# Queries and keys of heads 2 and 3 made by column block inside the attention, instead of in a second pass ahead of the values

## The chip, the cores and the metric

The kernel runs on one core of one Trainium2 chip. The metric is the device time of one execution in microseconds (us). Engines are named as in the profile: PE (TensorE), PEld (its weight loads), DVE (VectorE), ACT (ScalarE), POOL (GpSimd), SP (SyncE, which issues most of the DMAs). Lines such as L449 are lines of the kernel before; where a line belongs to the changed kernel, the text says so.

## What is computed

The reference is a network of two layers on 512 rows of x and 256 rows of ctx, 1024 features each. Only the mixer of the even layer is touched by the change. Cut to what matters, it is:

```python
u, v, q, k, vv = split(h @ w_in)            # h: normed and modulated rows; u, v, q, k, vv: 512 columns each
q, k = rope(q), rope(k)                     # 8 query and 8 key heads of 64 (rope on the rows of x only)
s = einsum(q, k) * HEAD_DIM ** -0.5
p = softmax(s)                              # 4 heads, each with two softmaxes
a = p[:, :, 0] - lam * p[:, :, 1]
o = a @ vv
y = concat([chunk_mlp(u, v), rmsnorm(o) * g]) @ w_out   # chunk_mlp: gelu, norm and mixing of blocks of 128 rows
```

The scale and shift that modulate h, and four more of each layer, come from products of a condition vector with a large matrix, `ada`.

## The kernel before

Every product is made in three matmuls (`mm3`, L106, L107, L108): the weight and the activation are both split into a high part and a rest, and hi*hi, hi*rest and rest*hi are summed. So each weight tile that comes by DMA (`unit`, L73) is cast on ACT (`CAST w<-raw`, L81), and POOL takes the rest (L84).

PSUM (where PE's results land) has eight banks. In this layer they are two `wide` tiles of two banks each (`pw` in the profile), three single banks (`pb`) and one bank called `fill` (`pf`). A new tile of one of these tags waits until all readers of the old one in its place are done.

The even layer, `even()`, goes on as follows. The numbers of time are those of the profiled execution.

- Start to 39.17 us: x, the first slabs of `ada`, norm.
- L449, loop `half`: for half 0 the queries and keys of heads 0 and 1, four blocks of 128 columns, all four at once over the eight tiles of the inner dimension: first for the 512 rows of x into two wide tiles, then for the 256 rows of ctx into two single banks. ACT moves them out (`evacuate`, L440). Then half 1, the same for heads 2 and 3 (81.28 to 122.24 us). Rope runs on DVE and POOL.
- L497 to L512: the values, eight tiles of the inner dimension with six accumulators each (122.24 to 162.87 us). ACT and DVE split them (`vhi`, `vlo`, L122 and L123).
- Sixteen slabs of `ada` (columns for j=2 and j=4, 1 MB each) are used on the side: `ada_ahead` issues the DMA, `ada_some` makes the eight small matmuls of one step (L359; the profile shows four or eight in a row), and after eight steps one copy on ACT (L366, `t`) and transposes (L368). Six steps stand in half 1, six in the values.
- Attention, `head(t)` for t = 0 to 3: three blocks of 256 rows, for each of which two `softmax_diff` of 128 rows are made. One of these takes two wide tiles: products (L542, L543, `pw<-kh,qa` and the like), row maximum on DVE (L544), exponential on ACT (L546, `e`), difference on DVE (L552). Then transposes (L564), their split on ACT and DVE (L122 `ath`, L123 `atl`) and the products with the values. The stacked and split queries and keys that a head needs (`stack`: L261, L262, L276, L277 on ACT, L265 and L279 on DVE) are made in the head before it.
- Filling: `gated(i)` makes one column block of u or v, 24 matmuls of 512 into the fill bank, a copy on ACT (L585), 24 of 256 into the same bank, a copy. The four blocks i = 4 to 7 (v) stand between the steps of heads 0 and 1. Their gelus (L632) are held behind the last exponential of head 1, since the two functions need different tables on ACT (`ACT_TABLE_LOAD`). Heads 2 and 3 are held behind the last gelu. They are filled by `turn(g)` (transposes of v, L644, copies, L645, and statistics, L648 and L649) and `gated(0)` to `gated(3)`, so `gated(0)` comes after the first `turn`.
- `mix` and the output product follow, then the feed-forward part and the odd layer, which the change leaves alone.

The order of the work on each engine is fixed when the program is built: a scheduler takes the ready instruction of highest priority. `tc.high_priority` sets a piece ahead of others, and `issue_after` holds it behind a named instruction. At run time each engine goes through its own list in order and waits for semaphores. SP's list of DMAs is such a list too, and a DMA waits there until the memory it writes is free.

Of the kernel before, what the change touches and what calls it, by code (L numbers as in the profile page):

```python
# [6 lines left out]
F32 = mybir.dt.float32  # L7
# [19 lines left out]
class Builder:  # L27
# [220 lines left out]
    def rope(self, ps, out, tabs):  # L248
        nc = self.nc
        sh = self.ropep.tile([P, 512], F32, name=self.uid("sh"), tag="sh", bufs=2)  # L250
# [71 lines left out]
    def even(self):  # L322
        tc, nc, a = self.tc, self.nc, self.a
        self.open_ring(512, 5, 6)
        self.adap = tc.alloc_tile_pool(name="ada0", bufs=1, side="left", reuse_waits="tile")
        self.ropep = tc.alloc_tile_pool(name="rope0", bufs=1, side="left", reuse_waits="tile")
# [111 lines left out]
        tabs = []  # L438

        def evacuate(ps, n, c, heads):  # L440
            h = heads[n % 2]
            key = h if n < 2 else 4 + h
            if key not in qk:
                qk[key] = f3()
            nc.scalar.mul(qk[key][:, c], ps, 0.125 if n < 2 else 1.0)
# [3 lines left out]
        for half, heads in enumerate(((0, 1), (2, 3))):  # L449
            w2 = [self.wide(), self.wide()]  # L450
            accx = [w[:, h * 512:(h + 1) * 512] for w in w2 for h in range(2)]
            W = []
            for k in range(KT):
                t = self.adap.tile([P, 2, 512], F32R, name=self.uid("wq"), tag="wq", bufs=3) if k % 3 == 2 else None
                with tc.issue_after(self.last_slab.ins) if half == 0 else ExitStack():
                    W.append(self.blocks(a["qk"][half, k], 512, t=t))
                    if half == 0:
                        if k > 4:
                            with tc.issue_after(self.last_w.ins):
                                ada_ahead(1)  # L460
                        if k == 7:
                            tabs += [self.load(self.ropep, a[n], [P, TX], n) for n in ("cos", "sin")]
                if half == 0:
                    t, sh = hx[k], self.modcol(0, 0, k, 0)
                    nc.scalar.activation(axx[k][0], t, AF.Identity, bias=sh)
                    nc.vector.scalar_tensor_tensor(axx[k][1], t, sh, axx[k][0].bitcast(F32), ALU.add, ALU.subtract)
                elif k % 2:
                    ada_ahead(1)
                    ada_some()
                for n in range(4):  # L470
                    self.mm3(accx[n], W[k][n], axx[k], k == 0, k == KT - 1)
                if half == 0 and k == 4:
                    rd = self.rstd_diag([(self.squares(hc, TC), TC)], 1.0 / D)[0]
                if half == 0 and k == 5:
                    rc = self.spread(rd)
                    for i in range(KT):
                        self.modulate(hc[i], TC, self.modcol(0, 1, i, 1), self.modcol(0, 0, i, 1), rc, axc[i])
            for n in range(4):
                evacuate(accx[n], n, slice(0, TX), heads)
            bk = [self.bank() for _ in range(2)]  # L480
            accc = [b[:, h * TC:(h + 1) * TC] for b in bk for h in range(2)]
            for k in range(KT):
                for n in range(4):
                    self.mm3(accc[n], W[k][n], axc[k], k == 0 and n % 2 == 0, k == KT - 1)
                if k % 2 and k > 2 - half:
                    ada_ahead(1)
                    ada_some()
            for n in range(4):
                evacuate(accc[n], n, slice(TX, TA), heads)
            for h in heads:  # L490
                for n in (h, 4 + h):
                    self.rope(qk[n][:, :TX], qk[n][:, :TX], tabs)
# [7 lines left out]
        for k in range(KT):  # L500
            W = self.unit(a["v0"][k * P:(k + 1) * P, :], 512)
            for tb in range(6):
                c = slice(tb * P, (tb + 1) * P)
                self.mm3(acc[tb], [t[:, c] for t in AX_[k]], W, k == 0, k == KT - 1)
            ada_ahead(1)
            ada_some()
# [12 lines left out]
        here = tc.cur_priority  # L519
        self.ropep.release()  # L520
# [10 lines left out]
        def softmax_diff(Q, K, qb, eps):  # L531
# [6 lines left out]
            for c in range(2):  # L538
# [6 lines left out]
                e = Ra.tile([P, TA], F32, name=self.uid("e"), tag="e", bufs=6)  # L545
# [120 lines left out]

        with tc.high_priority(offset=tc.cur_priority - here):
            QK = {0: stack(0)}
        for t in range(2):
            head(t)  # L670
# [12 lines left out]
        Ra.release()  # L683
        self.close_ring()
# [818 lines left out]
def prep(inp):  # L1503
# [18 lines left out]
    r["qk"] = c(ew[:, 1024:2048].reshape(KT, P, 2, 2, 2 * P).transpose(3, 0, 1, 2, 4).reshape(2, KT, P, 512))  # L1522
# [5 lines left out]

    r["uv"] = cols(ew[:, 0:1024])
# [44 lines left out]
```

## Time and profile before

| what | value |
|---|---|
| median of 3 runs | 1590.26 us (1588.08 to 1591.02) |
| profiled execution | 1588.33 us, its span 1586.3 us |
| mean granted clock of PE | 0.988 |
| PE busy | 1518.7 us (96%) |
| DVE, ACT, POOL busy | 1084.7, 723.3, 830.7 us |
| PE busy from 39 to 333 us (the span of the even mixer) | 275.60 us of 294.00 |

A table of windows shows, for each stretch, its length, the busy time of each engine with the number of its instructions in brackets, the granted clock of PE as a share of the full one, the busy share of the DMA engines and their GB/s. A table of waits has, for one engine, the instruction that waited and the one it waited for (after the arrow), the time in all, how often, and the longest. A timeline has the start, the length, engine, line and operation of each instruction with output and inputs, and in square brackets the idle time before it and what ended it.

### The profile page before, as it was taken

To read this page: it belongs to the slowest core of one execution; us is meant where nothing else is said; L and a number is where in the kernel's file an instruction comes from. 1 tells how busy PE (TensorE), PEld (TensorE's weight loads), DVE (VectorE), ACT (ScalarE), POOL (GpSimd) and SP (SyncE) were. 2 spreads that over 40 slices of the span, in tenths; PEclk is the share of its full clock that TensorE was granted. 3 is DMA by queue.
4 is the path that set the end of the run, shared out by engine and by line. 5 is a ranking of instruction groups with operands and counts; after the bars stand their busy time and mean duration, and the time that the engine had idled before them with its cause. 6 is when DMAs were issued, how large, how long until landed. Compare 5 with 4: busy or idle time off the path is not lost.

```text
span 1586.3 us, 24984 instructions
## 1 busy us (share of the span) xinstructions
PE 1518.7 (96%) x9547; PEld 1352.2 (85%) x9547; DVE 1084.7 (68%) x1958; ACT 723.3 (46%) x1472; POOL 830.7 (52%) x565
## 2 busy tenths in 40 slices
PE   6999988999999999999999989999999999999996
PEld 4776877889989999999999978777869989999996
DVE  4720788765688788888785585765667976666656
ACT  2412676553552333333333244565655644444443
POOL 0463211061256776677676415531304398888883
PEclk9999999999999999999999999999999999999998
DMA  8845100033223333454451012110225132323301
GB/s 328 308 145 188 40 8 1 3 131 133 67 80 113 114 120 106 140 166 147 164 165 57 27 52 80 61 34 14 68 80 206 54 120 88 113 92 109 94 14 54
DMA packets 54295, 162.00 MB, mean 102 GB/s; under 512 B 6176, under 2 KB 10656, under 8 KB 46496
## 3 DMA queue, kind: packets, MB, share of 16 engines
q1 hardware_dynamic: 47120, 135.11, 25.5%
q10 hardware_dynamic: 7056, 25.30, 4.9%
q8 instruction: 75, 1.23, 0.3%
q14 instruction: 44, 0.36, 0.1%
HBM read 158.29 MB, written 2.10 MB: 101 GB/s over the span
## 4 chain that ended last, share of the span: by engine, by line
PE 83%; DVE 10%; ACT 3%; issue 2%; DMA 1%; POOL 0%; POOLq 0%; SPq 0%; DVEq 0%; ACTq 0%
PE pw L106 11%; PE pw L107 11%; PE pw L108 11%; PE pb L107 8%; PE pb L106 8%; PE pb L108 8%; PE pf L106 4%; PE pf L107 4%; PE pf L108 4%; PE pb L1427 2%; PE pb L1416 2%; PE pf L359 2%; PE pw L1379 1%; PE pw L1387 1%; PE pw L542 1%
## 5 line engine op out<-in xcount | busy, mean ns | idle before, releaser
L84 POOL TENSOR_TENSOR w<-raw,w 128x512 fp32r<-128x512 f32 (+1 forms) x84 | 127.5, 1525 | 242.9 <-ACT w L81 220.5
L107 PE MATMUL pw<-ax,w 128*128 128x384 f32 (+2 forms) x732 | 233.9, 320 | 3.7 <-DVE ax L201 2.3
L106 PE MATMUL pw<-ax,w 128*128 128x384 f32 (+2 forms) x732 | 232.9, 322 | 4.1 <-DVE q L879 1.9
L108 PE MATMUL pw<-ax,w 128*128 128x384 f32 (+2 forms) x732 | 233.1, 320 | 0.1
L774 DVE SCALAR_TENSOR_TENSOR xT<-pb,mod,xT 128x512 f32<-128x512 f32 (+3 forms) x208 | 145.7, 707 | 125.8 <-PE pb L108 125.5
L879 POOL TENSOR_TENSOR w<-raw,w 128x512 fp32r<-128x512 f32 x110 | 169.4, 1555 | 19.7 <-ACT w L879 19.5
L879 POOL TENSOR_TENSOR w<-t,w 128x512 fp32r<-128x512 f32 x99 | 148.6, 1504 | 55.6 <-ACT w L879 55.6
L106 PE MATMUL pb<-hh,w 128*128 128x512 f32 x480 | 171.0, 356 | 2.3 <-DVE xT L774 2.3
L108 PE MATMUL pb<-hh,w 128*128 128x512 f32 x480 | 171.5, 357 | 0.3 <-DVE w L879 0.3
L107 PE MATMUL pb<-hh,w 128*128 128x512 f32 x480 | 171.1, 356 | 0.0
L107 PE MATMUL pw<-T,w 128*128 128x384 f32 (+1 forms) x508 | 156.9, 310 | 1.2 <-DVE T L123 1.2
L106 PE MATMUL pw<-T,w 128*128 128x384 f32 (+1 forms) x508 | 156.3, 310 | 1.1 <-DVE hs L879 1.1
L108 PE MATMUL pw<-T,w 128*128 128x384 f32 (+1 forms) x508 | 157.0, 310 | 0.0
L106 PEld LDWEIGHTS pw<-ax,w 128*128 128x128 f32 x732 | 138.5, 190 | 12.5 <-DVE q L879 2.6
L107 PEld LDWEIGHTS pw<-ax,w 128*128 128x128 f32 x732 | 139.0, 190 | 11.2 <-DVE ax L201 3.6
L106 PE MATMUL pf<-ax,w 128*128 128x256 f32 (+2 forms) x420 | 139.9, 333 | 7.9 <-DVE qf L252 5.0
L108 PEld LDWEIGHTS pw<-ax,w 128*128 128x128 f32 x732 | 139.2, 190 | 3.1 <-DVE w L948 0.4
L107 PE MATMUL pf<-ax,w 128*128 128x256 f32 (+2 forms) x420 | 138.8, 330 | 0.0
L108 PE MATMUL pf<-ax,w 128*128 128x256 f32 (+2 forms) x420 | 138.7, 330 | 0.0
L879 POOL TENSOR_TENSOR hh<-hs,hh 128x768 fp32r<-128x768 f32 (+1 forms) x42 | 80.7, 1922 | 90.0 <-ACT hh L879 67.6
L879 POOL TENSOR_TENSOR w<-rawo,w 128x512 fp32r<-128x512 f32 x59 | 103.5, 1754 | 30.1 <-ACT w L879 30.1
L228 DVE SCALAR_TENSOR_TENSOR junk<-ar,cb 128x1024 bf16<-128x1024 f32 x64 | 105.6, 1651 | 0.0
(378 smaller groups left out, 3936.8 us busy)
## 6 DMA issues: line engine op xcount, KB each, us to landing
raw<-ffn_in SPq DMA_DIRECT2D x44, 1024.0 KB, 5.1
ar<-ada SPq DMA_DIRECT2D x24, 1024.0 KB, 6.9
ar<-ada ACTq DMA_DIRECT2D x48, 512.0 KB, 3.5
rawo<-ffn_out SPq DMA_DIRECT2D x88, 256.0 KB, 3.0
raw<-odd_out SPq DMA_DIRECT2D x32, 256.0 KB, 2.7
raw<-qk SPq DMA_DIRECT2D x16, 256.0 KB, 7.9
raw<-uv SPq DMA_DIRECT2D x16, 256.0 KB, 2.7
raw<-even_out SPq DMA_DIRECT2D x8, 512.0 KB, 3.5
```

Source lines behind the costliest of these rows:

```text
L84: eng.tensor_tensor(lo, raw, hi.bitcast(F32), ALU.subtract)
L106: mm(out, s[0], m[0], start=start, stop=False, **kw)
L107: mm(out, s[0], m[1], start=False, stop=False, **kw)
L108: return mm(out, s[1], m[0], start=False, stop=stop, **kw)
L228: return self.nc.vector.scalar_tensor_tensor(junk, t, 1.0, self.cb[who], ALU.mult, ALU.mult, accum_out=self.acc[who][:, col:col + 1])
L359: nc.tensor.matmul(ps[32 * q:32 * q + 32, :w], cst[:, k, :], t[:, w * q:w * q + w], start=k == 0, stop=k == KT - 1, skip_group_check=True)
L542: nc.tensor.matmul(ps[:, :TX], Q[c][:, qs], K[c][p][:, :TX], start=p == 0, stop=p == 1)
L774: ins = self.nc.vector.scalar_tensor_tensor(h, ps[:, r], self.modcol(l, j, m, who), h, ALU.mult, ALU.add)
L879: tail[key] = fn(*args, **kw)
L1379: nc.tensor.matmul(ps[:, st:en], Q, K[g][p][:, b0 * P:b1 * P], start=p == 0, stop=p == 1, skip_group_check=True)
L1416: last = nc.tensor.transpose(pt[:, x * P:(x + 1) * P], es[2 * (x % 2) + x // 2][:, kb * P:(kb + 1) * P], self.ident)
L1427: nc.tensor.matmul(po[64 * h:64 * h + 64, :], V[vb][:, 64 * g:64 * g + 64], t[:, h * TC:h * TC + TC], start=kb == 0, stop=kb == nb - 1, sk ...
```

## The change

The loop over `half` is gone. What was half 0 stays, and the values follow it directly. Heads 2 and 3 get their queries and keys as four column blocks (order 2, 6, 3, 7: query of head 2, key of head 2, and so on), each made like a `gated` block: 24 matmuls of 512 into the fill bank, out by ACT (L445 of the changed kernel), 24 of 256, out by ACT, rope. They have lower priority than heads 0 and 1 and higher than `gated(4)` to `gated(7)`, so they are the first filling of heads 0 and 1. Weights are laid out to fit on the host, in `prep`. Twelve of the sixteen `ada` steps now stand in the values (one or two for each tile of the inner dimension), four in half 0. Since rope runs inside the attention, its tables and its buffer stay allocated until the attention is over, and three buffers are made smaller: `sh` from 2 to 1, `e` from 6 to 5, `wq` from 3 to 2. The numbers of instructions and of DMAs on each engine are the same as before.

```diff
-        for half, heads in enumerate(((0, 1), (2, 3))):
...
-                if half == 0:
-                    t, sh = hx[k], self.modcol(0, 0, k, 0)
...
-                elif k % 2:
-                    ada_ahead(1)
-                    ada_some()
...
+        keys = (0, 1, 4, 5)
+        W = []
+        for k in range(KT):
+            t = self.adap.tile([P, 2, 512], F32R, name=self.uid("wq"), tag="wq", bufs=2) if k in (2, 5) else None
+            with tc.issue_after(self.last_slab.ins):
+                W.append(self.blocks(a["qk"][k], 512, t=t))
+                if k > 3:
+                    with tc.issue_after(self.last_w.ins):
+                        ada_ahead(1)
...
@@ values
-            ada_ahead(1)
-            ada_some()
+            for _ in range(1 + k % 2):
+                ada_some()
+                ada_ahead(1)
...
-        here = tc.cur_priority
-        self.ropep.release()
         self.adap.release()
...
-                e = Ra.tile([P, TA], F32, name=self.uid("e"), tag="e", bufs=6)
+                e = Ra.tile([P, TA], F32, name=self.uid("e"), tag="e", bufs=5)
...
+        here = tc.cur_priority
+        for n, key in enumerate((2, 6, 3, 7)):
+            W = self.blocks(a["qk1"][n])
+            qk[key] = f3()
+            for c, A in ((slice(0, TX), axx), (slice(TX, TA), axc)):
+                ps = self.fill()[:, :c.stop - c.start]
+                self.dense(ps, W, A)
+                evacuate(ps, key, c)
+            self.rope(qk[key][:, :TX], qk[key][:, :TX], tabs)
         with tc.high_priority(offset=tc.cur_priority - here):
             QK = {0: stack(0)}
-        for t in range(2):
-            head(t)
+            for t in range(2):
+                head(t)
```

How the order moves is shown at three places. The numbers at the ends of names tell buffers apart and differ between the two kernels. First ACT at the end of the values, before: the last copy of `ada` (`t_1218`) and then the stacks of head 0 (`qa_1322` to `kh_1334`), and only then the values (`vhi`).

```order
L366 COPY t_1218<-pf_982 128x512
L261 ACTIVATE qa_1322<-f_102_572 64x768
L262 ACTIVATE qb_1323<-f_102_572 64x768
L276 CAST kh_1328<-f_104_576 64x768
L277 CAST kh_1328<-f_104_576 64x768
L261 ACTIVATE qa_1528<-f_103_574 64x768
L276 CAST kh_1334<-f_104_576 64x768
L277 CAST kh_1334<-f_104_576 64x768
L81 CAST w_2031<-raw_2029 128x512
L276 CAST kh_1534<-f_105_578 64x768
L277 CAST kh_1534<-f_105_578 64x768
L122 CAST vhi_1274<-pw_1045 128x512
```

The same place on ACT in the changed kernel, where `f_160` is the query block of head 2:

```order
L122 CAST vhi_1027<-pb_737 128x512
L81 CAST w_1197<-raw_1195 128x512
L122 CAST vhi_1019<-pw_735 128x512
L369 COPY t_997<-pf_863 128x512
L261 ACTIVATE qa_1326<-f_56_330 64x768
L262 ACTIVATE qb_1327<-f_56_330 64x768
L276 CAST kh_1332<-f_57_331 64x768
L277 CAST kh_1332<-f_57_331 64x768
L261 ACTIVATE qa_1532<-f_58_332 64x768
L276 CAST kh_1338<-f_57_331 64x768
...
L445 ACTIVATE f_160_1064<-pf_1065 128x512
...
L540 ACTIVATE e_1354,sa_1347<-pw_1348,sa_1346 128x768
```

The values' casts now stand ahead of the last `ada` copy and of the stacks, and the first evacuation of a filling product stands behind the stacks (three more rows of stacks stand in the first gap, one weight cast in the second).

Second, PE where the filling of head 1 ends. Before, the last four matmuls of `gated(7)` (`pf_2129`) have head 1's products with the values and its next scores behind them:

```order
L108 MATMUL pf_2129<-ax_323,w_2099 128x256
L106 MATMUL pf_2129<-ax_325,w_2099 128x256
L107 MATMUL pf_2129<-ax_326,w_2099 128x256
L108 MATMUL pf_2129<-ax_325,w_2099 128x256
L107 MATMUL pb_1651<-atl_1673,vhi_1282 128x256
L108 MATMUL pb_1651<-ath_1672,vlo_1283 128x256
L106 MATMUL pb_1651<-ath_1672,vhi_1286 128x256
...
L156 MATMUL pb_1699<-ones,sq_1601 128x128 x4
L543 MATMUL pw_1848<-kh_1534,qa_1528 128x256
```

In the changed kernel the last of `gated(7)` (`pf_2133`), then the transposes of `turn(0)` (L638) and the scores of head 2 (L536 and L537), the second pair of head 2's wide tiles:

```order
L107 MATMUL pf_2133<-ax_329,w_2103 128x256
L108 MATMUL pf_2133<-ax_328,w_2103 128x256
L638 MATMUL pf_2782<-ident_103,f_357_1917 128x128 x4
L536 MATMUL pw_2190<-kh_1832,qa_1826 128x512
L537 MATMUL pw_2190<-kh_1832,qa_1826 128x256
L536 MATMUL pw_2190<-kl_1833,qa_1826 128x512
L537 MATMUL pw_2190<-kl_1833,qa_1826 128x256
L536 MATMUL pw_2198<-kh_1838,qb_1827 128x512
```

No product of head 1 is left behind `gated(7)`: from there to `gated(0)` stand six transposes of `turn(0)`, one of head 2 and the scores of five wide tiles.

Third, ACT at the same place. Before, the four gelus stand together behind the last exponential of head 1 and well behind `gated(7)`'s copy (`f_375` from `pf_2129`, 12 rows ahead of that exponential):

```order
L546 ACTIVATE e_1877,sa_1866<-pw_1873,sa_1865 128x256
L632 ACT_TABLE_LOAD
L632 ACTIVATE f_354_1913<-f_354_1913 128x768
...
L632 ACTIVATE f_375_2102<-f_375_2102 128x768
L261 ACTIVATE qa_2378<-f_139_885 64x768
L276 CAST kh_2384<-f_141_889 64x768
...
L122 CAST ath_1811<-pb_1806 128x512
L546 ACT_TABLE_LOAD
L546 ACTIVATE e_2169,sa_2162<-pw_2163,sa_2161 128x768
```

In the changed kernel, where the copy of `gated(7)`'s second part comes just ahead of the last gelu:

```order
L579 COPY f_378_2106<-pf_2133 128x256
L81 CAST w_2981<-raw_2979 128x512
L626 ACTIVATE f_378_2106<-f_378_2106 128x768
L540 ACT_TABLE_LOAD
L540 ACTIVATE e_2173,sa_2166<-pw_2167,sa_2165 128x768
L540 ACTIVATE e_2181,sa_2166<-pw_2175,sa_2165 128x768
L261 ACTIVATE qa_2382<-f_176_1200 64x768
L276 CAST kh_2388<-f_184_1268 64x768
...
L639 COPY f_357_1917<-pf_2782 128x512
L540 ACTIVATE e_2196,sa_2189<-pw_2190,sa_2188 128x768
L540 ACTIVATE e_2204,sa_2189<-pw_2198,sa_2188 128x768
L540 ACTIVATE e_2297,sa_2290<-pw_2291,sa_2289 128x768
```

The first exponentials of head 2 now follow directly on the end of the filling, with the gelu and the table load between.

More of the change, by code (lines that the diff above doesn't have):

```diff
@@ L436, in ctx_load, with evacuate @@
                 hc.extend(t[:, n, :] for n in range(4))
[L438 to L445, printed above, removed]
+        for key in (0, 4, 1, 5):
+            qk[key] = f3()
+        def evacuate(ps, key, c):
+            nc.scalar.mul(qk[key][:, c], ps, 0.125 if key < 4 else 1.0)
         with tc.issue_after(self.last_slab.ins):
@@ new lines, in even @@
+        for n in range(4):
+            evacuate(accx[n], keys[n], slice(0, TX))
+        bk = [self.bank() for _ in range(2)]
+        accc = [b[:, h * TC:(h + 1) * TC] for b in bk for h in range(2)]
+        for k in range(KT):
+            for n in range(4):
+                self.mm3(accc[n], W[k][n], axc[k], k == 0 and n % 2 == 0, k == KT - 1)
+            if k % 2:
+                ada_some()
+                ada_ahead(1)
+        for n in range(4):
+            evacuate(accc[n], keys[n], slice(TX, TA))
@@ L493, in even @@
+        for n in (0, 4, 1, 5):
+            self.rope(qk[n][:, :TX], qk[n][:, :TX], tabs)
         Rh.release()
@@ L1527, in cols @@
         return c(w.reshape(KT, P, n, P).transpose(2, 1, 0, 3).reshape(n, P, KT * P))
+    r["qk1"] = cols(c(qk[:, :, 1].reshape(D, 2, 2, P).transpose(0, 2, 1, 3).reshape(D, 512)))
     r["uv"] = cols(ew[:, 0:1024])
```

66 lines of the change are left out of this document (27 added, 39 removed).

## The prediction

> **What bounds the kernel now.** I read the page's head and its chain first, to see which engine the time belongs to.
>
> ```profile
> span 1586.3 us, 24984 instructions
> ...
> PE 1518.7 (96%) x9547; PEld 1352.2 (85%) x9547; DVE 1084.7 (68%) x1958; ACT 723.3 (46%) x1472; POOL 830.7 (52%) x565
> ...
> PE 83%; DVE 10%; ACT 3%; issue 2%; DMA 1%; POOL 0%; POOLq 0%; SPq 0%; DVEq 0%; ACTq 0%
> ```
>
> PE is busy for 96% of the span and carries 83% of the chain. Its instructions are not fewer after the change, so the change can only gain or lose PE's idle time and slow clock. The order of the two kernels differs only from about 64 us on, and is again the same from the output product of the even layer on, so I cut the even mixer into stages with a table of windows: half 0, half 1, values, attention until the last filling block `gated(7)` ends, then until `gated(0)` starts, then the rest.
>
> ```profile
> 39.17:81.28 42.11, 40.45 (x230) 30.98 (x231) 28.94 (x51) 20.25 (x39) 21.18 (x15) 1.00 0.78 291
> 81.28:122.24 40.96, 40.96 (x247) 30.66 (x245) 10.04 (x20) 8.72 (x19) 27.80 (x21) 1.00 0.48 161
> 122.24:162.87 40.63, 40.63 (x200) 28.00 (x197) 7.19 (x10) 12.44 (x18) 13.55 (x11) 1.00 0.45 162
> 162.87:224.20 61.33, 57.73 (x356) 50.54 (x355) 47.03 (x82) 38.55 (x81) 13.12 (x9) 1.00 0.10 31
> 224.20:252.25 28.05, 21.79 (x106) 17.67 (x105) 24.14 (x67) 22.10 (x42) 3.11 (x2) 0.76 0.00 0
> 252.25:333.00 80.75, 74.04 (x477) 64.17 (x474) 62.97 (x204) 50.75 (x104) 10.53 (x7) 1.00 0.10 34
> ```
>
> Half 1 and the values have no idle PE at all (40.96 of 40.96, 40.63 of 40.63). In the fourth stage, where filling stands between the steps of heads 0 and 1, PE idles 61.33 - 57.73 = 3.60 us. In the fifth, without filling, it idles 28.05 - 21.79 = 6.26 us, and its clock is 0.76. The clock steps of that stage show what the slow clock costs.
>
> ```profile
> 227.22:230.63 3.41, 1.20 (x7) 0.61 (x5) 3.31 (x8) 2.86 (x6) 0.00 (x0) 1.00 0.00 0
> 230.63:234.05 3.42, 2.83 (x10) 2.34 (x11) 3.33 (x13) 2.45 (x8) 0.00 (x0) 0.50 0.00 0
> 234.05:237.46 3.41, 3.41 (x16) 3.22 (x15) 2.52 (x10) 3.38 (x5) 0.00 (x0) 0.50 0.00 0
> 237.46:240.87 3.41, 1.48 (x12) 1.20 (x11) 2.89 (x5) 3.36 (x6) 1.53 (x1) 1.00 0.00 0
> 240.87:244.29 3.42, 2.71 (x4) 1.34 (x5) 3.37 (x7) 3.39 (x6) 0.28 (x1) 0.50 0.00 0
> 244.29:247.70 3.41, 3.41 (x12) 2.89 (x11) 3.28 (x14) 0.77 (x2) 0.00 (x0) 0.50 0.00 0
> ```
>
> A step in which PE was busy for 1.20 or 1.48 of 3.41 us is followed by half clock. Four half steps hold 2.83 + 3.41 + 2.71 + 3.41 = 12.36 us of busy PE, of which half, 6.2 us, is lost. So from the end of the values to `gated(0)` the kernel loses 3.60 + 6.26 + 6.2 = **16.1 us**. This is what the change puts at stake: it brings four more filling blocks.
>
> **The change, part by part.** *Half 1 goes.* Its six `ada` steps are 48 matmuls, eight in 1.06 us as the timeline has them, so about 1.0 us each in a row.
>
> ```profile
> L359 PE MATMUL pf<-ar,cst 128*32 128x512 f32 x48 | 6.4, 605 | 0.0
> ```
>
> Half 1 is 40.96 us, less 6.0 for these steps and 0.5 for their transposes: 34.4 us of products. The six steps move to the values, which go from 40.6 to about 47.1 us, and the products become filling. So the attention starts at 162.87 - 34.4 = 128.5 us. The same products are made again there, into the fill bank, in the same matmul sizes: 34.4 us. The two cancel, and the transition to `gated(0)` would be reached at the old time if as much were lost as before. By the order, one more pair of scores (0.7 us) stands ahead of `gated(0)` in the changed kernel. So the break-even is a loss of 16.1 + 0.7 - 0.7 = 16.1 us between the end of the values and `gated(0)`. The sum below is the new loss.
>
> *Start of the attention.* Before, the stacks of head 0 are made during the values, beside a full PE:
>
> ```profile
> 154.22 0.59 ACT L366 COPY t<-pf 128x512 f32<-128x512 f32 x1 [0.36 <-PE pf L359]
> 154.71 0.84 ACT L261 ACTIVATE qa<-f 64x768 fp32r<-64x768 f32 x1
> 155.57 0.84 ACT L262 ACTIVATE qb<-f 64x768 fp32r<-64x768 f32 x1
> 156.44 0.83 ACT L276 CAST kh<-f 64x768 fp32r<-64x768 f32 x1
> 157.30 0.83 ACT L277 CAST kh<-f 64x768 fp32r<-64x768 f32 x1
> ```
>
> After, the last `ada` step stands at the end of the values, the copy that frees its fill bank stands behind six casts of the values, and nine stack instructions of 0.83 to 0.84 us stand ahead of the first evacuation. The last step's copy cannot start earlier than the casts end (I find PE 0.85 us idle), and nine stacks are 7.6 us, where the first filling product gives 5.6 us of cover and the first scores some more: 1.1 us idle. Together **1.95 us**.
>
> *Filling of heads 0 and 1.* Filling blocks have one bank, so each ends with a wait for its copy. What this costs when ACT is occupied is seen here, the copy standing behind two stack casts:
>
> ```profile
> 200.86 0.84 ACT L276 CAST kh<-f 64x768 fp32r<-64x768 f32 x1
> ...
> 201.72 0.83 ACT L277 CAST kh<-f 64x768 fp32r<-64x768 f32 x1
> ...
> 202.57 0.58 ACT L585 COPY f<-pf 128x512 f32<-128x512 f32 x1
> ...
> 203.21 0.39 PE L106 MATMUL pf<-ax,w 128*128 128x256 f32 x1 [1.34 <-ACT f L585]
> ```
>
> Following both lists in the changed order, I find such a wait behind the stacks of head 1 (1.4 us), one of a score product's split behind the six `L173` of the norm (1.25 us; six are 2.82 us in the trace), one at `gated(7)`, whose second part stands directly behind its first (0.9 us), and two of 0.3 us: 4.15 us. Hand-walking misses small ones; the 3.60 us before for four blocks would be 7.2 us for eight, and 1.95 + 4.15 = 6.1 is a little under this, so I add 1.1 and take **7.2 us** in all until `gated(7)` ends (bounds: 3.6, as before, and twice 7.2).
>
> *Transition to head 2.* This is the large term. Before, 224.20 to 252.25 us holds the rest of head 1 as cover (28.05 us with 21.79 busy). After, no product of head 1 is left when `gated(7)` ends (call it T), and to `gated(0)` only 4.1 us of PE work remain: six transposes, five score groups of 0.70 us (from start to start in the timeline) and one more transpose. Between them stands a chain on ACT and DVE, whose members the trace has:
>
> ```profile
> 234.13 1.28 ACT L632 ACT_TABLE_LOAD   x1
> 235.43 3.05 ACT L632 ACTIVATE f<-f 128x768 f32<-128x768 f32 x4
> ...
> 242.70 0.90 ACT L546 ACTIVATE e<-pw,sa 128x768 f32<-128x768 f32 x1
> ...
> L544 DVE TENSOR_REDUCE sa<-pw 128x1 f32<-128x768 f32 x23 | 21.6, 950 | 9.9 <-PE pw L543 9.7
> L279 DVE TENSOR_TENSOR kl<-f,kh 64x768 fp32r<-64x768 f32 x14 | 14.1, 1011 | 0.2
> L552 DVE SCALAR_TENSOR_TENSOR e<-e,sa,e 128x768 f32<-128x768 f32 x11 | 12.3, 1115 | 0.2
> ```
>
> ACT after T: copy 0.4, weight cast 0.6, gelu 0.8, table load 1.3, two exponentials of 0.9: T + 5.0. DVE then has, in its order, two reduces (1.9), a small step (0.3), the difference (1.0 to 1.1), two `kl` (1.9 to 2.0), four statistics (0.9), small steps (0.2), the third reduce (0.95): T + 12.1 to 12.4. Then the fifth score group waits for the next exponential (0.9) and takes 0.7: `gated(0)` starts at T + 13.5 to 14.6, I take T + 14.0. Lost: 14.0 - 4.1 = **9.9 us** (bounds 8 and 12: one reduce out of the chain, or one pair more in it).
>
> *Clock.* The steps in this stretch are mostly idle, so half clock follows, as above. Of the 4.1 us of work only the last score group lies on the chain (+0.7), and `gated(0)` may start in a half step (up to 1.7 lost). I take **1.6 us** (0 to 3.4). The Trainium skill ("TensorE: Matmul & The Clock Gate", section "What's actually happening") lets the clock fall only after a wholly idle window of about 3.4 us. The trace differs: a step with 1.20 of 3.41 us busy was enough. By the rule the term would be nearer 0.7, and the sum 0.9 us lower.
>
> *The rest.* The buffers made smaller stand on tiles that no wait above runs through: I cost them at 0, hidden by PE's own work in the values and filling; with that cover gone, an `e` too few costs one exponential, 0.9 us, each time. From 252.25 us on the order is the same, and I take 0, plus or minus 1.
>
> **Sum.** 7.2 + 9.9 + 1.6 = 18.7 us lost instead of 16.1: +2.6 us. On the profiled execution 1588.33 + 2.6 = 1590.9. The median of the runs, 1590.26, lies 1.9 us over that execution, so in its terms **1592.8**.
>
> **The rivals.**
>
> *Faster: the filling covers.* Four more blocks lie over heads 0 and 1, where DVE and ACT had 47.03 and 38.55 of 61.33 us. The same head work spread over some 105 us leaves both idle half the time, so waits for `e`, `ath` and `atl` (1.4 + 0.5 + 0.4 = 2.3 of the 3.6 us) may vanish. These are PE's waits from 162.87 to 224.20 us:
>
> ```profile
> PE pw L542 <- ACT e L546: 1.4, 1, 1.4
> PE pf L106 <- ACT f L585: 1.3, 1, 1.3
> PE pb L106 <- ACT ath L122: 0.5, 2, 0.2
> PE pb L107 <- DVE atl L123: 0.4, 1, 0.4
> ```
>
> If 3.6 is lost until T and the transition costs 8 without clock, the loss is 11.6: -4.5 us, **1585.8**. For it speaks the table; against it, that the waits named above are waits behind instructions in ACT's list, which idle time elsewhere doesn't shorten. It decides where head 1 has products left when `gated(7)` ends.
>
> *No change.* The small terms stay at what I walked (6.1) and the transition takes T + 13.5 with half a microsecond of clock: 6.1 + 9.4 + 0.5 = 16.0, **1590.2**.
>
> *Slower still: one fill bank.* All eight parts of the new blocks queue in the one bank that `gated` uses too, where before they had the wide tiles and single banks. If each of the eight costs what one cost at 203.21 (1.34), that is 10.7 instead of the 3.6 I have for half the blocks: +7.1 on the sum less half of what is already counted, about +4 more, **1597**. The Trainium skill ("Perfetto Trace Analysis", "Optimizing Tensor Performance") says that independent groups of matmuls should rotate through PSUM banks so that the evacuation of one overlaps the next; the change does the opposite. Here other matmuls stand between most parts, and of the eight parts before only one was followed by such a wait (the second row just above), so I don't take it.
>
> *Slower: the values wait for DMA.* Twelve slabs of 1 MB are wanted in 47 us, besides 2 MB of values' weights and the new blocks' weights:
>
> ```profile
> 40.00:60.00 20.00, 18.44 (x78) 13.42 (x79) 13.87 (x21) 7.27 (x13) 10.86 (x8) 1.00 0.93 348
> ...
> 120.00:140.00 20.00, 20.00 (x105) 13.17 (x105) 0.00 (x0) 4.25 (x9) 10.51 (x9) 1.00 0.85 313
> ```
>
> I reckon about 15 MB between 62 and 116 us, 277 GB/s, under the 313 and 348 seen. Four slab buffers and SP's list, in which slabs stand behind weights that wait for the ring, could lower the rate; at 250 GB/s the values end 6 us late, **1599**.
>
> *The change doesn't do what it says*: the blocks aren't used as filling. The order shows them between the scores of heads 0 and 1, so I give it nothing.
>
> **How the numbers follow.** My forecast, 1590.5 to 1597 with 1592.8 as its value, has 0.5; faster 0.2; no change 0.1; one of the two slower ones 0.2. A measurement here tells about 0.2% (3.2 us) from no change, so I put the forecast's own half at 0.25 over and 0.25 under 1593.5. So slower 0.25 + 0.2 = 0.45, within 0.25 + 0.1 = 0.35, faster 0.2. The range leaves out the ends of the outer cases: 1585.5 to 1600.5.
>
> **What would show it.** The start of the attention's filling at about 128.5 us, with two idle spells of PE around 1 us near it; `gated(7)` ending near 237; then a window of 13 to 15 us with some 4 us of PE busy and a clock under 0.8; `gated(0)` near 255. PE idle in the values would show the DMA rival; waits of `pf` L106 for the evacuations of 7 us and more would show the bank rival; a transition window of under 11 us, or products of the values standing in it, the faster one. Wrong altogether would be a difference that lies behind 333 us.

## The result, and the profile after

| | before | changed |
|---|---|---|
| median of 22 runs each | 1589.19 us (1585.91 to 1591.86) | 1592.48 us (1588.65 to 1595.27) |
| profiled execution, its span | 1588.33, 1586.3 us | 1590.09, 1588.3 us |
| PE's mean granted clock | 0.988 | 0.988 |

The ratio is 1.0015, with a 95% interval of 1.0009 to 1.0021: the change costs 1.4 to 3.3 us. The forecast was 1592.8 us.

The head of the page after the change says next to nothing. PE is as busy as before:

```profile
span 1588.3 us, 24991 instructions
...
PE 1517.7 (96%) x9547; PEld 1352.1 (85%) x9547; DVE 1090.5 (69%) x1958; ACT 723.5 (46%) x1472; POOL 830.8 (52%) x565
```

So the stages are read again. These windows of the changed kernel run from the first products of queries and keys to the values, to the start of filling, to the end of `gated(7)`, to the start of `gated(0)`, and to the first output product of the even layer. Columns as before; the second number is PE's busy time, the last but two its clock.

```profile
39.17:80.81 41.64, 39.55 (x233) 30.85 (x232) 25.31 (x49) 19.66 (x38) 19.90 (x14) 1.00 0.76 281
80.81:129.50 48.69, 47.98 (x251) 29.56 (x249) 9.53 (x17) 10.92 (x21) 21.92 (x17) 1.00 0.63 227
129.50:237.66 108.16, 103.05 (x631) 90.45 (x629) 78.54 (x142) 63.60 (x122) 32.61 (x23) 1.00 0.12 35
237.66:253.32 15.66, 8.06 (x27) 5.84 (x28) 10.89 (x26) 11.69 (x21) 3.69 (x3) 0.66 0.01 2
253.32:336.14 82.82, 75.64 (x470) 64.50 (x470) 60.56 (x200) 47.72 (x99) 10.50 (x6) 0.98 0.10 32
```

The attention's filling starts 33.4 us earlier (129.50 against 162.87), lasts 46.8 us longer (108.16 against 61.33) and PE idles for 5.11 us in it, 4.7% where it was 3.60 of 61.33, 5.9%. Then comes a hole: of 15.66 us PE is busy for 8.06, at a clock of 0.66. A timeline of PE shows it (the waits stand in square brackets):

```profile
238.12 0.66 PE L638 MATMUL pf<-ident,f 128*128 128x128 f32 x4 [0.46 <-ACT f L579]
241.69 0.50 PE L536 MATMUL pw<-kh,qa 128*128 128x512 f32 x1 [2.91 <-ACT e L540]
...
247.06 0.47 PE L558 MATMUL pb<-ident,e 128*128 128x128 f32 x1 [2.87 <-DVE e L546]
...
251.88 0.80 PE L536 MATMUL pw<-kh,qa 128*128 128x512 f32 x1 [1.36 <-ACT e L540]
...
253.32 0.63 PE L106 MATMUL pf<-ax,w 128*128 128x512 f32 x1
```

And the same time on ACT, with the gelu, the table load and the two exponentials that PE waits for:

```profile
237.70 0.37 ACT L579 COPY f<-pf 128x256 f32<-128x256 f32 x1 [0.77 <-PE pf L108]
237.97 0.62 ACT L81 CAST w<-raw 128x512 fp32r<-128x512 f32 x1
238.49 0.85 ACT L626 ACTIVATE f<-f 128x768 f32<-128x768 f32 x1
239.35 1.28 ACT L540 ACT_TABLE_LOAD   x1
240.64 0.90 ACT L540 ACTIVATE e<-pw,sa 128x768 f32<-128x768 f32 x1
```

The clock over the hole and behind it, in the half steps 242.63 to 256.28, divided where `gated(0)` starts:

```profile
242.63:253.32 10.69, 6.46 (x20) 4.75 (x20) 10.64 (x25) 6.79 (x13) 1.81 (x1) 0.50 0.01 2
253.32:256.28 2.96, 2.96 (x8) 2.32 (x8) 2.44 (x8) 0.99 (x2) 0.00 (x0) 0.50 0.00 0
```

For the comparisons below a measure is wanted that repeats. Total times don't repeat well: the waits of the first products (around 42 us) differ by 1.1 us between two executions of one kernel, and what follows the even mixer, from its first output product to the start of the last product of the program, took 1244 to 1252 us in the profiles, as more or fewer half-clock steps fell into it (last section). So I take the time from the first product for the rows of ctx in half 0 to the first output product, called **the stretch** here. Before, its ends are these rows, 268.22 us apart; in the changed kernel they start at 64.23 and 336.14 us, 271.91 apart.

```profile
64.70 0.39 PE L106 MATMUL pb<-ax,w 128*128 128x256 f32 x1
...
332.92 0.42 PE L106 MATMUL pw<-ax,w 128*128 128x384 f32 x1
```

The stretch leaves one thing out. From the first product of queries and keys to its start both kernels have the same 112 matmuls, but the order differs from 48.6 us on, not only from 64 us on as the prediction reads it. They take 24.50 us in the changed kernel and 25.53 in the kernel before. So the change gains 1.0 us ahead of the stretch: over the stretch it costs 3.7 us, from the first product on 2.7.

### The profile page after: what moved, and what is told of

Same layout as the page of the kernel before. It is cut to its first block, busy times and chain, and to the rows that moved or that the text cites. A ratio compares the mean times of both kernels' runs of the same rounds, so it can differ in the third digit from the quotient of the medians.

```text
span 1588.3 us, 24991 instructions
## 1 busy us (share of the span) xinstructions
PE 1517.7 (96%) x9547; PEld 1352.1 (85%) x9547; DVE 1090.5 (69%) x1958; ACT 723.5 (46%) x1472; POOL 830.8 (52%) x565
## 4 chain that ended last, share of the span: by engine, by line
PE 72%; DVE 8%; ACT 3%; issue 1%; POOL 0%; POOLq 0%; ACTq 0%; DVEq 0%
PE pw L108 10%; PE pw L106 10%; PE pw L107 10%; PE pb L108 8%; PE pb L107 8%; PE pb L106 8%; PE pf L106 3%; PE pf L107 3%; PE pf L108 3%; PE pb L1432 2%; PE pb L1421 2%; PE pw L1384 1%; PE pw L1392 1%; DVE t L884 1%; DVE T L123 1%
## 5 line engine op out<-in xcount | busy, mean ns | idle before, releaser
L106 PE MATMUL pw<-ax,w 128*128 128x384 f32 (+2 forms) x708 | 223.5, 319 | 4.1 <-DVE q L884 1.9
L107 PE MATMUL pw<-ax,w 128*128 128x384 f32 (+2 forms) x708 | 224.3, 318 | 2.7 <-DVE ax L465 1.4
L108 PE MATMUL pw<-ax,w 128*128 128x384 f32 (+2 forms) x708 | 223.7, 317 | 0.1
L106 PE MATMUL pf<-ax,w 128*128 128x256 f32 (+2 forms) x484 | 163.2, 337 | 10.9 <-DVE qf L252 6.3
L108 PE MATMUL pf<-ax,w 128*128 128x256 f32 (+2 forms) x484 | 161.1, 333 | 0.0
L107 PE MATMUL pf<-ax,w 128*128 128x256 f32 (+2 forms) x484 | 160.4, 331 | 0.0
L106 PEld LDWEIGHTS pw<-ax,w 128*128 128x128 f32 x708 | 134.0, 190 | 9.7 <-DVE q L884 2.6
L107 PEld LDWEIGHTS pw<-ax,w 128*128 128x128 f32 x708 | 134.7, 190 | 8.4 <-DVE ax L201 2.4
L108 PEld LDWEIGHTS pw<-ax,w 128*128 128x128 f32 x708 | 134.6, 190 | 2.1 <-DVE w L953 0.4
L106 PEld LDWEIGHTS pf<-ax,w 128*128 128x128 f32 x484 | 92.4, 191 | 19.6 <-DVE qf L252 3.8
```

The lines of the kernel that those rows point to most:

```text
L106: mm(out, s[0], m[0], start=start, stop=False, **kw)
L107: mm(out, s[0], m[1], start=False, stop=False, **kw)
L108: return mm(out, s[1], m[0], start=False, stop=stop, **kw)
```

## The experiments

All twelve runs in one table. The ratio is against the kernel before, on the same chip, with its 95% interval. The stretch is from the profile.

| kernel | median, us | ratio to before | stretch, us |
|---|---|---|---|
| before, changed (given) | 1589.19, 1592.48 | 1.0015 (1.0009 to 1.0021) | 268.2, 271.9 |
| before_again, after_again | 1591.07, 1591.15 (one run each) | | 268.4, 271.5 |
| cover_after | 1600.02 | 1.0057 (1.0045 to 1.0069) | 273.8 |
| cover_before | 1600.71 | 1.0069 (1.0055 to 1.0083) | 276.0 |
| late3 | 1587.10 | 0.9984 (0.9975 to 0.9992) | 266.1 |
| ada_early | 1594.04 | 1.0023 (1.0014 to 1.0032) | 271.3 |
| drop_k7 | 1587.81 | 0.9975 (0.9964 to 0.9987) | 263.7 |
| drop_g1 | 1599.27 | 1.0045 (1.0026 to 1.0064) | 275.3 |
| drop_before | 1595.70 | 1.0025 (1.0014 to 1.0035) | 269.2 |
| before_bufs | 1596.60 | 1.0031 (1.0019 to 1.0043) | 270.2 |
| before_e5 | 1594.03 | 1.0021 (1.0012 to 1.0031) | 270.0 |
| before_sh1 | 1593.26 | 1.0017 (1.0007 to 1.0027) | 268.0 |

**Does the stretch repeat?** after_again and before_again are the two kernels unchanged.

> The changed kernel once more. Theory: its stretch from the first product of queries and keys to the output product of the even layer repeats within 0.7 us of 296.4; the half-clock steps behind it lie on another grid of 3.41 us, so their number and the total differ. Rival: the stretch itself varies by as much as the difference between the kernels (2.7 us).

> The kernel before once more. Theory: the same stretch within 0.7 us of 293.75, the number of later half-clock steps differs from four. Rival: the stretch itself varies by 2 us or more.

From the first product of queries and keys the two executions of the changed kernel took 296.4 and 297.1 us, those of the kernel before 293.75 and 295.0, the last outside the 0.7 us that I had expected. The difference lies ahead of the ctx part. From there they took 271.9 and 271.5, and 268.2 and 268.4. So the change costs the stretch 3.1 to 3.7 us, and 2.1 to 2.7 us from the first product on. With two executions of each kernel, 0.1 and 0.4 us apart, I take a difference of one microsecond in the stretch as readable.

**Cover in the transition.** My theory was that the hole between heads 1 and 2 is what the change loses, and that products put there are gained. `gated(0)` needs no gelu; it is put ahead of `turn(0)`, in both kernels:

```diff
         for g in range(4):
+            if g == 0:
+                gated(g)
             turn(g)
-            gated(g, after if g == 3 else None)
+            if g > 0:
+                gated(g, after if g == 3 else None)
```

> The changed kernel with gated(0) put ahead of turn(0), so that its 48 products (8.4 us), which need no gelu, stand in the transition to head 2. Theory (the change loses by an uncovered transition: 15.7 us with some 4 us of work at full clock): 6 to 9 us less than the changed kernel, so 4 to 7 us less than the kernel before; the stretch from the end of gated(7) to the first product after gated(0)'s is nearly free of idle time. Rival (the one fill bank: its copies queue on ACT behind exponentials, whatever stands in it): at most 2 us less. Second rival (heads 2 and 3 are bound by ACT and DVE, so what is used up here is missed later): 0 to 3 us less, with new idle time of PE behind 290 us.

> The kernel before with the same edit, gated(0) ahead of turn(0). Theory: it lost 12.5 us in its own transition (6.3 idle, 6.2 by half clock), so it too gains, 6 to 9 us, and the difference between the two kernels stays within 2 us of what it was. Rival (the kernel before has the rest of head 1 as cover and its loss there is a chain on ACT and DVE that cover doesn't help): at most 3 us, and the changed kernel with the edit becomes the faster one by 2 us or more.

Both became slower, by 1.9 to 2.4 us (changed kernel) and 7.6 to 7.8 us (before) in the stretch. In cover_after the hole was filled as meant. The first three windows are of the changed kernel, transition, head 2 and up to the output product:

```profile
237.00:253.00 16.00, 8.40 (x32) 6.07 (x31) 10.57 (x25) 11.69 (x21) 4.35 (x3) 0.68 0.00 1
253.00:290.00 37.00, 34.80 (x207) 29.71 (x207) 27.79 (x78) 19.02 (x42) 4.60 (x3) 0.96 0.00 1
290.00:336.14 46.14, 41.16 (x267) 35.02 (x266) 33.08 (x123) 28.70 (x58) 5.90 (x3) 1.00 0.17 58
```

And the same of cover_after:

```profile
237.00:253.00 16.00, 14.47 (x86) 12.22 (x85) 8.05 (x12) 11.36 (x20) 5.46 (x4) 1.00 0.00 1
253.00:290.00 37.00, 32.59 (x209) 27.78 (x208) 34.54 (x109) 24.09 (x53) 5.30 (x3) 1.00 0.01 1
290.00:339.35 49.35, 39.02 (x223) 32.76 (x222) 27.85 (x106) 24.15 (x49) 5.43 (x3) 0.90 0.15 54
```

The transition idles 1.53 us instead of 7.60, at full clock. But then idle time grows from 2.20 to 4.41 and from 4.98 to 10.33 us, and the clock falls to 0.90 in the last window. My theory of the cure fell: the second rival holds, and more strongly than it was put (0 to 3 us less; it was 2 more). Filling for heads 2 and 3 is a fixed stock of four blocks, and what is used up in the transition is missed at the end. PE's waits in cover_after behind 252 us are those of a head without filling, on exponentials, splits and the square of the last norm:

```profile
PE pb L106 <- ACT ath L122: 3.4, 3, 2.0
PE pb L156 <- ACT sq L595: 3.2, 1, 3.2
PE pw L536 <- ACT e L540: 2.5, 2, 1.3
PE pb L107 <- DVE atl L123: 1.6, 2, 1.3
```

In cover_before the hole hardly shrinks and the rest idles twice as long. Its windows are the transition of the kernel before and what follows up to the output product:

```profile
224.20:252.25 28.05, 22.97 (x140) 20.05 (x139) 23.00 (x54) 22.09 (x40) 6.02 (x5) 0.94 0.00 1
252.25:342.11 89.86, 75.54 (x452) 65.40 (x450) 65.64 (x219) 51.03 (x106) 7.42 (x4) 0.92 0.08 30
```

PE idles 5.08 us instead of 6.26, and then 14.32 instead of 6.71. Neither account of cover_before expected a loss, so both fell; only the rival's remark that the changed kernel with the edit is the faster of the two, by 2 us or more, came true in the stretch (2.2 us).

**What a filling product costs, by place.** The new theory: heads 0 and 1 of the changed kernel have more filling than they need, so a product costs its full length there, while heads 2 and 3 have too little, so products there cost little or nothing. To test it, 42 of the 48 products of one block are left out, 7.4 us of PE work, once in heads 0 and 1 (the key block of head 3), once in heads 2 and 3 (`gated(1)`), and once in heads 0 and 1 of the kernel before (`gated(5)`):

```diff
-                self.dense(ps, W, A)
+                self.dense(ps, W[:1] if key == 7 else W, A)
...
-                self.dense(ps, W, A, after, 0 if off else 2)
+                self.dense(ps, W[:1] if i == 1 else W, A, after, 0 if off else 2)
```

> The changed kernel with 42 of the 48 products of one new column block (the key block of head 3, last of the four) left out, 7.4 us of PE work in heads 0 and 1; its weights, evacuations and rope stay. Theory (heads 0 and 1 are bound by PE and filled to the brim, so what is put there costs its full length): 6 to 8 us less than the changed kernel. Rival (ACT and DVE set the pace of heads 0 and 1, and filling is nearly free there): less than 4 us.

> The changed kernel with the same number of products (42 of 48, 7.4 us) left out of gated(1), which fills heads 2 and 3; all else stays. Theory (heads 2 and 3 have too little filling and are bound by ACT and DVE): at most 3 us less than the changed kernel, idle time of PE takes the place of the products. Rival (PE binds there as in heads 0 and 1): 6 to 8 us less.

> The kernel before with 42 of the 48 products of gated(5) left out, 7.4 us in its heads 0 and 1. Theory: with four blocks its filling already ends before head 1 does, so fewer products only make the bare end longer: 2 to 5 us less than the kernel before, clearly less than the same cut saves in the changed kernel. Rival (PE binds there too): 6 to 8 us less.

In heads 0 and 1 of the changed kernel leaving them out saves 7.8 to 8.2 us of the stretch, a little over its full length. In heads 2 and 3 it costs 3.4 to 3.8 us: less work, and more time. In the kernel before it costs 0.8 to 1.0, where both accounts expected a gain, of 2 to 5 or of 6 to 8 us. The windows of drop_g1, against those of the changed kernel above, show where it goes:

```profile
253.00:290.00 37.00, 32.57 (x204) 27.99 (x204) 30.85 (x93) 22.50 (x49) 3.31 (x2) 0.99 0.00 1
290.00:338.52 48.52, 37.91 (x224) 32.89 (x223) 27.93 (x103) 24.50 (x49) 5.44 (x3) 0.86 0.16 55
```

Idle time is 4.43 + 10.61 = 15.0 us instead of 2.20 + 4.98 = 7.2, which is the 7.4 us of products given back as waits. On top, the clock is 0.86 in the last window. Over the whole stretch, with half of PE's busy time in half steps counted as lost to the clock, PE idles 8.0 us more, loses 3.8 us more to the clock and is busy for 8.3 us less. In drop_before it idles 4.4 us more, loses 3.3 us more to the clock and is busy for 6.8 us less. The direction of the theory holds in the changed kernel; that the price of filling is below nothing in two places was not expected. In all three kernels the scheduler also puts many instructions of the heads in another order when a block is shorter. No run separates this from the products themselves, so the prices are those of one block each, with the new order in them.

**Head 3's blocks later.** If filling is too much in heads 0 and 1 and too little behind them, some of the new blocks belong behind. Head 3's query and key are first needed in the second block of head 2. In late3 their two column blocks are made behind `gated(7)`, in priority below head 2:

```diff
-        for n, key in enumerate((2, 6, 3, 7)):
+        for key in (2, 6, 3, 7):
+            qk[key] = f3()
...
+        late(0, 2)
+        late(1, 6)
...
             last = gelu(i, self.last_exp)
+        late(2, 3)
+        late(3, 7)
         with tc.high_priority(offset=tc.cur_priority - here), tc.issue_after(last.ins):
             head(2)
```

> The changed kernel with the two column blocks of head 3 put behind gated(7) in priority, as filling from the end of head 1 into head 2, instead of at the start. Theory (uncovered transition): 17 us of products that need no gelu stand there, the transition's loss falls from 11.6 to 2 or 4 us: 6 to 9 us less than the changed kernel. Rival (one fill bank): no more than 2 us less, the waits for evacuations only move. Second rival (filling used up early in heads 2 and 3 is missed later): it can't hold here, since the filling is more, not moved from later.

The stretch is 266.1 us, 5.4 to 5.8 less than the changed kernel and 2.2 less than before; the total is 0.08% to 0.25% below the kernel before. It is the fastest kernel here that leaves nothing out. Its windows, transition to output product:

```profile
237.00:253.00 16.00, 13.15 (x82) 12.20 (x82) 15.25 (x34) 11.26 (x23) 6.21 (x4) 0.79 0.01 2
253.00:290.00 37.00, 34.35 (x217) 29.95 (x217) 29.37 (x86) 21.21 (x48) 4.55 (x3) 1.00 0.00 1
290.00:331.52 41.52, 34.90 (x210) 29.37 (x208) 22.81 (x97) 21.87 (x40) 5.50 (x3) 0.96 0.18 64
```

The windows are the same times, not the same work: in late3 `gated(7)` ends at 211.42 us and the last of head 3's blocks at 241.03. PE idles for 2.85 us in the first instead of 7.60, and in the later ones together for 9.27 instead of 7.18. So the later stages idle a little longer here too, but by less than the hole loses, and over the stretch PE idles 16.8 us instead of 20.6. The gain fell a little short of the 6 to 9 us. The clock's part hardly fell (4.6 us instead of 4.7): two half steps stay in the transition and one lies near 315 us. Against the kernel before, whose stretch has 16.6 us of idle time, late3 idles no less; it loses 1.6 us less to the clock.

**The start of the attention.** The twelve `ada` steps of the values are brought forward, so that the stacks of head 0 can start before the values end:

```diff
-            for _ in range(1 + k % 2):
+            for _ in range((2, 2, 2, 2, 2, 1, 1, 0)[k]):
```

> The changed kernel with the twelve ada steps of the values at two for each of the first five tiles, one for the next two, none for the last, so that the stacks of head 0 can be made beside the last products. Theory: the two idle spells at the start of the attention (0.71 and 1.08 us) go: 1.5 to 2 us less than the changed kernel. Rival (slabs of ada can't come so early): PE waits for slabs within the values, the same or up to 5 us more.

The stretch is 271.3 us, 0.2 to 0.6 less. The two waits (0.71 and 1.08 us) became one, of about their sum:

```profile
138.01 0.39 PE L106 MATMUL pf<-ax,w 128*128 128x256 f32 x1 [2.12 <-ACT f L445]
```

The first five stacks now stand ahead of the values' casts on ACT and the other four among them, and the first evacuation is behind both, as in the changed kernel. From the last `ada` copy at 125.71 us to that evacuation at 137.34 ACT waits for nothing, so PE waits for the sum of its work there; starting one step earlier is not enough. The rival fell too: PE waits for no slab, though all slabs come earlier. (The total, 1594.04 us, is no less than the changed kernel's; its profile has two more half-clock steps behind 1200 us.)

**The smaller buffers.** They are made in the kernel before, alone, and then apart (only the line of `e` is shown):

```diff
-                e = Ra.tile([P, TA], F32, name=self.uid("e"), tag="e", bufs=6)
+                e = Ra.tile([P, TA], F32, name=self.uid("e"), tag="e", bufs=5)
```

> The kernel before with the three smaller buffers of the change alone (sh 1, e 5, wq 2 at tiles 2 and 5 of the inner dimension). Theory (they cost nothing): within 2 us of the kernel before. Rival (one buffer of exponentials fewer holds exponentials back): 3 us more or worse, seen as waits of ACT for the transposes.

> The kernel before with one buffer of exponentials fewer (e 5 instead of 6) and nothing else. The three smaller buffers together cost 2.0 us up to the output product of the even layer (295.8 against 293.75 from the first product of queries and keys). Theory: e is the one that costs, through the order in heads 2 and 3: 2 us more there. Rival: sh or wq: nothing here.

> The kernel before with sh 1 and wq 2 alone, e left at 6. Theory: nothing, within 0.5 us up to the output product. Rival (rope through one buffer is late for the stacks, or weights wait for their place): the 2 us are here.

Together they cost 1.9 to 2.0 us of the stretch, `e` alone 1.6 to 1.8, the two others nothing (268.0; the total of before_sh1 is longer all the same, by what lies behind the stretch). So the theory of no cost fell, and `e` is the one that costs. With five buffers a wait of PE appears in head 3 that the kernel before doesn't have at that place:

```profile
299.07 0.38 PE L107 MATMUL pb<-atl,vhi 128*128 128x256 f32 x1 [1.46 <-DVE atl L123]
```

The order of these heads on PE, ACT and DVE changes with the number of buffers, and this wait is on a split, not on an exponential. But the sign that the rival named is there too: an exponential waits for PE's transposes, which read the older exponentials. The row of before_e5 is

```profile
281.53 0.90 ACT L546 ACTIVATE e<-pw,sa 128x768 f32<-128x768 f32 x1 [1.21 <-PE pb L564]
```

before_bufs has it with 1.3 us; before, before_again and before_sh1, all with six buffers, have no such wait of 0.2 us or more behind 252 us. So a full buffer is seen as well as another order, and which of the two makes up the 1.6 to 1.8 us stays open. Six buffers in the changed kernel were not tried.

## Why the prediction was right, point by point

- **Start of the attention at 128.5 us.** It was 129.50 including a wait of 0.71. Half 0 ended 0.5 us earlier than before (80.81 against 81.28), and the values with twelve `ada` steps took 47.98 us of PE time (47.1 forecast).
- **Waits at the start, 0.85 and 1.1 us.** Measured 0.71 and 1.08, with the releasers named (`t` L369, the evacuation L445).
- **Waits while filling, 7.2 us with the start.** Measured 0.71 + 5.11 = 5.82. The wait behind head 1's stacks (1.4) was 1.25, that of `gated(7)` 0.89 (0.9). The one that I placed behind the norm's `L173` (1.25) did not appear with more than 0.44. The term was 1.4 too large. These are PE's waits from 129.50 to 237.66 us in the changed kernel:

```profile
PE pf L106 <- ACT f L445: 2.3, 2, 1.2
PE pf L106 <- ACT f L579: 0.9, 1, 0.9
PE pw L536 <- ACT e L540: 0.6, 2, 0.3
PE pb L107 <- DVE atl L123: 0.4, 1, 0.4
```

- **Transition: `gated(0)` at T + 14.0, of which 9.9 us lost, and 1.6 for the clock.** T was 237.66 (near 237 was forecast), and `gated(0)` started at T + 15.66. In the hole PE idles for 7.60 us, and half of the 6.46 us in half steps, 3.2, is slow clock; behind it `gated(0)` loses half of 2.96, 1.5. Together 12.3 us, against 9.9 + 1.6 = 11.5: too little by 0.8. The rows show where the chain was longer. Its third reduce ended at T + 13.1 instead of T + 12.1 to 12.4, because the small step on DVE, for which the sum has 0.3 us, took 1.63; and the last score group took 1.44 us at half clock, the 0.7 more that the clock's term allows. The half clock of the other groups doesn't set the length: after_again has 1.9 us of it in the hole instead of 3.2, with 8.50 us idle instead of 7.60, and its transition takes 15.43 us. The small step stood beside a product of POOL:

```profile
243.57 1.63 DVE L545 SCALAR_TENSOR_TENSOR sa<-sa,nlam,sa 128x1 f32<-128x1 f32 x1
243.39 1.81 POOL L265 TENSOR_TENSOR qa<-f,qa 64x768 fp32r<-64x768 f32 x1 [3.46 <-ACT qa L261]
```

Most of these small steps take 0.2 us. Each one of them up to 345 us that began beside a running product of POOL, six in the changed kernel and one in the kernel before, ended within 0.02 us of that product's end. The sum has no term for this.
- **Sum, 18.7 us against 16.1.** It is 5.8 + 12.3 = 18.1. The misses of -1.4 and +0.8 partly cancel. Of the 3.7 us in this pair of profiles, 2.0 are so accounted for, 0.5 are more idle time in the last stage (82.82 - 75.64 = 7.18 against 80.67 - 73.96 = 6.71 from `gated(0)` to the output product). The remaining 1.2 us are PE's busy time, with the clock's part taken out (246.6 us of the stretch against 245.5). I had costed that at 0, and what it is stays open: late3, which makes the same products in the same bank, has 244.7 us of it and ada_early 245.2, so longer products there don't explain it. The second pair of profiles differs by 3.1 us in another way: 6.3 us more idle time, 4.8 us less lost to the clock, 1.6 us more busy.

- **The rest, 0 plus or minus 1.** It came to +0.7, within its bounds by balance: 1.0 us gained ahead of the stretch, against the 0.5 and the 1.2 above. The cost of nothing for the buffers did not hold: in the kernel before, `e` at 5 costs 1.6 to 1.8 us. In the changed kernel exponentials wait for transposes twice behind 253 us, 2.6 us in all (0 in the kernel before), but ACT is not what PE always waits for, and of the cost no more can be seen than the 0.5 us of more idle time in the last stage.
- **A pair of scores more ahead of `gated(0)`.** I counted 0.7 us for it and against it. It did move: behind the start of `gated(0)` the changed kernel has 18 score products of 512 columns and 34 of 256, the kernel before 20 and 36. Yet the last stage, without its 1.5 us of half clock, has 74.2 us of PE work against 74.0 before, so 0.9 us of the open 1.2 lies there.
- **Median.** 1588.33 + 2.6 + 1.9 = 1592.8 was reckoned on a median of 1590.26; over 22 runs it is 1589.19. So the base was 1.1 us too high. The medians differ by 3.3 us, the ratio of 1.0015 means 2.4, and 2.6 were forecast. That 1592.8 lies only 0.3 us from the measured median is luck.
- **Rivals.** *DMA*: PE waits for no slab or weight in the values; the 0.71 us of idle time there is the wait for the copy on ACT. *One fill bank*: waits of `pf` for copies are 2.3 + 0.9 = 3.2 us up to T, in three waits, not 10.7. The rule of the Trainium skill on rotating banks ("Perfetto Trace Analysis", section "Optimizing Tensor Performance") speaks against the change, but the trace shows it costing little here, as head products stood between most parts. *The filling covers*: its condition, products of head 1 behind `gated(7)`, is not met, and the hole is there. *No change*: the 22 runs tell the two kernels apart, though the ratio of 1.0015 is less than the 0.2% that I had taken as the bound.

The prediction was right about the hole, its place and nearly its size, but it did not see that filling such a hole need not help. It priced idle time place by place. The drops, of one block each, show that products have a price by place: about their full length in heads 0 and 1 of the changed kernel, nothing or less in heads 2 and 3. The change moved 34.4 us of products from one place where they cost their full length (half 1, 40.96 of 40.96 us busy) to another, so there was little to gain, and the hole and the waits for copies came on top.

## What to carry to other kernels

Filling is a stock: before moving products in as filling, ask of each stage whether PE or the other engines set its pace, and give the products to the stage where PE idles, even if a nearer place looks convenient. In these kernels a hole that was filled with what a later stage would have used only moved (cover_after); filled with work from a stage that was full of PE anyway, it was gained in the main (late3, 5.4 to 5.8 us less than the changed kernel). When small differences are to be read, take a stretch of the trace that repeats, not the total.

## What the runs showed of the hardware

- PE at half clock has the same length of step in every profile, 3.41 us, on a grid that lies differently in each. Behind the output product four to eight such steps fell into the profiles (before 4 and 6, changed 4 and 4, before_bufs 8), always at three to six of the same six places (around 135, 603, 652, 850, 867 and 942 us behind the first output product), and that part took 1244 to 1252 us up to the start of the last product. In the 14 profiles here, 79 steps at full clock had PE busy for under 45% of their 3.41 us, and each was followed by a half step; of 55 steps with 45 to 57% 20 were, and of the fuller ones none. So whether an idle spell costs a half step depends on where the grid cuts it. before_again, with one step more at 1273.7 us, took 1.5 us longer over that place than before. Why the totals of some kernels stay longer over all their runs, with the same stretch or a little more (before_sh1, before_bufs, ada_early), isn't settled by these runs.
- Leaving out products can make a kernel slower (drop_g1, drop_before), in part by the clock. Ahead of the output product seven half steps fell into each of their profiles, against four or five in those of the kernel before and two or four in those of the changed kernel. Where PE has filling to spare this doesn't show: drop_k7, with as many products left out, has one.
